# A two-layer hybrid decoder trunk on one core: the inverse norms of K and Q move from VectorE's bit estimate to GpSimd's power

## The chip, the cores and the metric

The kernel runs on one core of a Trainium2 chip. The metric is the time of one execution on the device in microseconds (us). The kernel before takes 1410.69 us, the median of three runs (1410.56 to 1411.05).

The core's engines run side by side, each through a queue of its own in order: TensorE (PE; its weight loads are shown as PEld), VectorE (DVE), ScalarE (ACT), GpSimd (POOL) and SyncE (SP), which here issues the DMAs. They wait for each other by semaphores.

## The reference

Two decoder layers on 512 tokens of width 1024. The first mixes with a state-space scan (SSD) and a stick-breaking attention of 16 heads, the second with an mLSTM; each is followed by a gated feed-forward with a convolution. The change lies in the attention's normalisation of Q and K: every head vector of 64 numbers is divided by its root mean square.

```
def rmsnorm(x, w):
    y = x * rsqrt(mean(x * x, axis=-1) + 1e-6)
    return y * w

heads = lambda t: t.reshape(bsz, seq, 16, 64)
qh = rmsnorm(heads(q), q_norm_w)
kh = rmsnorm(heads(k), k_norm_w)
vh = heads(v)
y_sb = stick_breaking(qh, kh, vh)      # z = qh kh^T / 8, strictly causal
```

## The kernel before, in words

All matrix products are done on float32 split in a high and a low part (`split`, `split_scaled`, and `prefetch` for the weights): ScalarE rounds to the high part, VectorE subtracts to get the remainder (`lo`, `wTl`, `Kl`), and TensorE does three products of the parts. So nearly every product needs VectorE shortly ahead of it.

The attention's projections are done in eight groups of two heads (`kqv`). A group projects the normalised input to K, Q and V, token block by token block (4 blocks of 128), and puts K and Q into two tiles `kqs` of 128x512: four token blocks, each with two heads of K and two of Q, 64 columns a head. Then come the inverse norms, 16 for each of 128 tokens. ScalarE squares (`sq`), VectorE sums each 64 columns (`ss`, 128x16), adds the epsilon, and `rsqrt` takes ss to the power -1/2: it shifts the bits of ss as an integer, subtracts from a constant, and does three Newton steps of three instructions each, twelve instructions of 128x16 on VectorE. VectorE multiplies the two kqs tiles with the result `f`, TensorE transposes them (`tt<-cc,kqs`), ScalarE and VectorE take the transposes apart into `Kh`, `Kl` and `Q`, and one half of Kl is copied to other partitions by a DMA on SyncE's queue.

Two other functions (`rstd`, used by the norms, and `ml_core` of the second layer) already take an inverse root as a GpSimd power with the constant tile `mhalf`, four columns at a time.

What is written down is not what is issued. Every call goes into a `Recorder`. Its `order` then plays the whole program through with a price for each call (`cost`) and a delay for each hand-over between engines (`LATENCY` plus `SLACK`), and the calls are issued in the order of the start times that come out: one fixed order for each engine. A GpSimd call is priced at 60 + 2n ns (n columns), a VectorE call at 69 + about n ns, with 127 ns more to a call on VectorE that needs its result; a hand-over to or from GpSimd costs 150 + 200 ns. So a change in a few calls can move any later instruction on any engine.

`L0_PLAN` says what is woven together in the first layer: groups 0 to 2 stand beside the convolution tiles and the scan's heads (`ssd`), groups 3 to 7 beside the attention (`att`, the function `sb_pair`) of the groups before them. In the attention a pair of heads takes sigmoids on ScalarE, cuts the diagonal blocks with GpSimd's select (`wt<-wt`), runs a scan (`gt`) and a product (`wt`) on VectorE, transposes on TensorE and splits the result (`wTh`, `wTl`).

Weights come through two buffers `raw` and are split into five buffers `hi` and `lo`, so up to five units of weights are ready ahead of TensorE.

Of the kernel before, what the change touches and what calls it, by code (L numbers as in the profile page):

```python
# [15 lines left out]
F32 = mybir.dt.float32  # L16
F32R = mybir.dt.float32r
AF = mybir.ActivationFunctionType
ALU = mybir.AluOpType
# [3 lines left out]
P = 128  # L23
# [411 lines left out]
class Net:  # L435
# [107 lines left out]
        for k in range(KD):  # L543
            self.mm3(ps[:, 0:n], (xs[k][0][:, t], xs[k][1][:, t]), ws[k], k == 0, k == KD - 1)

    def rsqrt(self, y, x, n):

        v, I32 = self.nc.vector, mybir.dt.int32
        b, m = self.sm("nb", n), self.sm("nm", n)
        v.tensor_scalar(y.bitcast(I32), x.bitcast(I32), 1, None, op0=ALU.logical_shift_right)  # L550
        v.tensor_scalar(y.bitcast(I32), y.bitcast(I32), -1, 0x5F3759DF, op0=ALU.mult, op1=ALU.add)
        v.tensor_scalar(m, x, -0.5, None, op0=ALU.mult)
        for _ in range(3):
            v.tensor_tensor(b, y, y, op=ALU.mult)
            v.tensor_tensor(b, b, m, op=ALU.mult)
            v.scalar_tensor_tensor(y, b, 1.5, y, op0=ALU.add, op1=ALU.mult)


    def sumsq_add(self, acc, src, first):
        if first:  # L560
# [203 lines left out]
    def kqv(self, xs, ev, r, pr, dt=None, ws=None):  # L764


        nc, v = self.nc, self.nc.vector
        ws = ws or self.tok_units()
        st = [self.slot("kqs"), self.slot("kqs")]
        V = [self.slot("V", F32R), self.slot("V", F32R)]  # L770
        raw = [self.slot("Vr"), self.slot("Vr")] if dt is not None else None
        for tb in range(NB):
            ps = self.ps()
            self.tok_block(ps, xs, ws, tb)
            o = (tb % 2) * 256
            nc.scalar.copy(st[tb // 2][:, o : o + 256], ps[:, 0:256])
            rt, src = r[:, tb : tb + 1], ps[:, 256:384]
            if raw:
                both = raw[tb // 2][:, o : o + P + 16]
                nc.scalar.copy(both, ps[:, 256 : 384 + 16])  # L780
                src = both[:, 0:P]
                v.scalar_tensor_tensor(dt[:, tb * 16 : tb * 16 + 16], both[:, P : P + 16], rt, self.param("rows", 0, 16), op0=ALU.mult, op1=ALU.add)
            src = self.v3(src, 2)
            vh, vl = (V[tb // 2][:, o : o + 256].rearrange("p (e s c) -> p e s c", e=2, s=2)[:, :, k] for k in range(2))
            nc.scalar.activation(vh, src, AF.Copy, scale=rt)
            v.scalar_tensor_tensor(vl, src, rt, vh.bitcast(F32), op0=ALU.mult, op1=ALU.subtract)
            yield
        ss, f = self.sm("ss", 16), self.sm("f", 16)
        for j in range(2):
            sq = self.slot("sq")  # L790
            nc.scalar.activation(sq, st[j], AF.Square)
            v.tensor_reduce(ss[:, 8 * j : 8 * j + 8], self.v3(sq, 8), axis=AX.X, op=ALU.add)
        v.scalar_tensor_tensor(self.v3(ss, NB), self.v3(ss, NB), 1.0 / 64, ev.unsqueeze(2).broadcast_to([P, NB, 4]),
                               op0=ALU.mult, op1=ALU.add)
        self.rsqrt(f, ss, 16)
        for j in range(2):
            v.tensor_tensor(self.v3(st[j], 8), self.v3(st[j], 8), f[:, 8 * j : 8 * j + 8].unsqueeze(2).broadcast_to([P, 8, 64]), op=ALU.mult)
        yield
        pk, pq = self.ps("tt"), self.ps("tt")
        for k, pt in enumerate((pk, pq)):  # L800
            for tb in range(NB):
                o = (tb % 2) * 256 + k * P
                self.transpose(pt[:, tb * P : (tb + 1) * P], st[tb // 2][:, o : o + P])
        KL, K, Q = [], [], []
        for e in range(2):
            own, other = slice(e * 64, e * 64 + 64), slice(64 - e * 64, P - e * 64)
            kh, kl, q = self.slot("Kh", F32R), self.slot("Kl", F32R), self.slot("Q", F32R)
            nc.scalar.copy(kh[own], pk[own])
            nc.scalar.copy(kh[other], pk[own])
            v.tensor_tensor(kl[own], pk[own], kh[own].bitcast(F32), op=ALU.subtract)  # L810
            nc.sync.dma_start(kl[other].bitcast(F32), kl[own].bitcast(F32))
            KL.append(kl)
            nc.scalar.activation(q[own], pq[own], AF.Copy, scale=self.wqk[own])
            v.scalar_tensor_tensor(q[other], pq[own], self.wqk[own], q[own].bitcast(F32), op0=ALU.mult, op1=ALU.subtract)
            K.append(kh)
            Q.append(q)
        self.kqv_of[pr] = (K, KL, Q, V)
        yield
# [340 lines left out]

    def run(self):  # L1160
        nc = self.nc
        self.mhalf = self.const.tile([P, 8], F32, name="mhalf")
        nc.vector.memset(self.mhalf, -0.5)
        warm = self.slot("warm", F32R)
        nc.gpsimd.memset(warm.bitcast(F32), 0.0)
# [117 lines left out]
        a, b, c = L1_CUTS  # L1283
# [78 lines left out]
```

## Time and profile before

| | |
|---|---|
| median of three runs | 1410.69 us |
| the profiled execution | 1410.06 us |
| its span, from the first to the last instruction | 1408.3 us |
| TensorE busy | 1397.9 us (99%) |
| VectorE busy | 989.2 us (70%) |
| ScalarE busy | 742.3 us (53%) |
| GpSimd busy | 58.9 us (4%) |
| share of the chain that ended last | TensorE 88%, VectorE 5%, ScalarE 3% |

The busy share of an engine is the time in which at least one of its instructions was being executed. VectorE's instructions overlap a little: the next begins before the last has ended. A busy TensorE can still hide short waits, since its instructions are pipelined and their ends are modelled. All lines of the recorded calls have the number of the one line that issues them, L422, so the groups are told apart by the names of their tiles.

### The profile page before, as it was taken

To read this page: it belongs to the slowest core of one execution; us is meant where nothing else is said; L and a number is where in the kernel's file an instruction comes from. 1 tells how busy PE (TensorE), PEld (TensorE's weight loads), DVE (VectorE), ACT (ScalarE), POOL (GpSimd) and SP (SyncE) were. 2 spreads that over 40 slices of the span, in tenths; PEclk is the share of its full clock that TensorE was granted. 3 is DMA by queue.
4 is the path that set the end of the run, shared out by engine and by line. 5 is a ranking of instruction groups with operands and counts; after the bars stand their busy time and mean duration, and the time that the engine had idled before them with its cause. 6 is when DMAs were issued, how large, how long until landed. Compare 5 with 4: busy or idle time off the path is not lost.

```text
span 1408.3 us, 18392 instructions
## 1 busy us (share of the span) xinstructions
PE 1397.9 (99%) x6915; PEld 1170.1 (83%) x6915; DVE 989.2 (70%) x1659; ACT 742.3 (53%) x1229; POOL 58.9 (4%) x140
## 2 busy tenths in 40 slices
PE   9999999999999999999999999999999999999998
PEld 8898999989788888888888898888888888888887
DVE  7999889999987676677623347799767777675221
ACT  7798987886665444444422236685444444443110
POOL 0000001211120000000000000010000000000000
PEclk9999999999999999999999999999999999999999
DMA  6423323234213223323233225232223223223330
GB/s 217 128 76 120 91 61 101 65 91 150 83 31 120 90 90 99 96 90 104 83 98 94 72 76 170 70 109 78 85 90 105 90 90 103 93 86 105 109 102 33
DMA packets 44393, 135.27 MB, mean 96 GB/s; under 512 B 5112, under 2 KB 6136, under 8 KB 44304
## 3 DMA queue, kind: packets, MB, share of 16 engines
q1 hardware_dynamic: 44304, 134.09, 30.5%
q8 instruction: 54, 0.88, 0.3%
q14 instruction: 35, 0.29, 0.1%
HBM read 128.78 MB, written 2.15 MB: 93 GB/s over the span
## 4 chain that ended last, share of the span: by engine, by line
PE 88%; DVE 5%; ACT 3%; issue 3%; DMA 1%; POOL 0%; SPq 0%; DVEq 0%; POOLq 0%; ACTq 0%
PE pj L422 42%; PE yy L422 20%; PE zz L422 17%; PE tt L422 8%; DVE gt L422 1%; DVE wt L422 1%; DVE lo L422 1%; DVE wTl L422 1%; DMA E<-mrow 0%; ACT L422 0%; ACT E L422 0%; ACT Kh L422 0%; POOL wt L422 0%; DMA w<-in_w 0%; ACT Q L422 0%
## 5 line engine op out<-in xcount | busy, mean ns | idle before, releaser
L422 ACT CAST hi<-raw 128x1024 fp32r<-128x1024 f32 (+2 forms) x236 | 234.7, 997 | 269.5 <-PE pj L422 75.9
L422 DVE TENSOR_TENSOR lo<-raw,hi 128x1024 fp32r<-128x1024 f32 (+2 forms) x236 | 272.4, 1156 | 135.3 <-ACT hi L422 135.0
L422 PE MATMUL pj<-xnh,hi 128*128 128x512 f32 x544 | 216.8, 398 | 0.0
L422 PE MATMUL pj<-xnh,lo 128*128 128x512 f32 x544 | 215.9, 397 | 0.0
L422 PE MATMUL pj<-xnl,hi 128*128 128x512 f32 x544 | 215.4, 396 | 0.0
L422 DVE SCALAR_TENSOR_TENSOR c<-u,pp,c 128x511 f32<-128x511 f32 (+2 forms) x212 | 158.0, 748 | 3.5 <-ACT c L422 0.5
L422 PEld LDWEIGHTS pj<-xnh,lo 128*128 128x128 f32 x544 | 102.3, 188 | 22.1
L422 PEld LDWEIGHTS pj<-xnl,hi 128*128 128x128 f32 x544 | 102.3, 188 | 21.4
L422 PEld LDWEIGHTS pj<-xnh,hi 128*128 128x128 f32 x544 | 102.3, 188 | 21.3 <-issue 0.2
L422 PE MATMUL pj<-lo,xnh 128*128 128x384 f32 (+2 forms) x320 | 108.6, 340 | 0.0
L422 PE MATMUL pj<-hi,xnl 128*128 128x384 f32 (+2 forms) x320 | 107.2, 335 | 0.0
L422 PE MATMUL pj<-hi,xnh 128*128 128x384 f32 (+2 forms) x320 | 106.8, 338 | 0.0
L422 PE MATMUL zz<-xnh,lo 128*128 128x512 f32 x224 | 88.4, 394 | 0.0
L422 PE MATMUL yy<-xnh,lo 128*128 128x512 f32 x224 | 88.4, 394 | 0.0
L422 PE MATMUL yy<-xnh,hi 128*128 128x512 f32 x224 | 88.3, 394 | 0.0
L422 PE MATMUL zz<-xnh,hi 128*128 128x512 f32 x224 | 88.3, 394 | 0.0
L422 PE MATMUL yy<-xnl,hi 128*128 128x512 f32 x224 | 88.2, 394 | 0.0
L422 PE MATMUL zz<-xnl,hi 128*128 128x512 f32 x224 | 88.2, 394 | 0.0
L422 ACT CAST sh<-c 128x512 fp32r<-128x512 f32 x44 | 27.3, 620 | 113.5 <-DVE c L422 113.5
L422 ACT ACTIVATE c<-c 128x512 f32<-128x512 f32 x56 | 35.3, 631 | 96.9 <-DVE c L422 96.8
L422 ACT ACTIVATE c<-u,pp 128x512 f32<-128x512 f32 x100 | 81.4, 816 | 1.2 <-DVE u L422 0.9
L422 DVE TENSOR_TENSOR u<-pj,rb 128x512 f32<-128x512 f32 x44 | 30.4, 691 | 48.4 <-PE pj L422 44.2
(363 smaller groups left out, 2977.2 us busy)
## 6 DMA issues: line engine op xcount, KB each, us to landing
raw<-in_w SPq DMA_DIRECT2D x184, 512.0 KB, 3.6
raw<-in_w SPq DMA_DIRECT2D x44, 384.0 KB, 3.1
h<-in_xT SPq DMA_DIRECT2D x16, 256.0 KB, 4.4
E<-acsd SPq DMA_DIRECT2D x16, 256.0 KB, 4.0
raw<-in_w SPq DMA_DIRECT2D x8, 264.0 KB, 2.7
Kl<-Kl SPq DMA_DIRECT2D x16, 128.0 KB, 2.2
E<-mrow SPq DMA_DIRECT2D x8, 256.0 KB, 5.4
out_h<-h SPq DMA_DIRECT2D x8, 256.0 KB, 2.0
```

The source lines that it names most:

```text
L422: getattr(getattr(nc, c.engine), c.method)(*(r(a) for a in c.args), **{k: r(v) for k, v in c.kw.items()})
```

## The change

The method `rsqrt` is taken out, the one call of it is replaced by a single GpSimd instruction, and the constant tile becomes 16 columns wide.

```diff
-    def rsqrt(self, y, x, n):
-
-        v, I32 = self.nc.vector, mybir.dt.int32
-        b, m = self.sm("nb", n), self.sm("nm", n)
-        v.tensor_scalar(y.bitcast(I32), x.bitcast(I32), 1, None, op0=ALU.logical_shift_right)
-        v.tensor_scalar(y.bitcast(I32), y.bitcast(I32), -1, 0x5F3759DF, op0=ALU.mult, op1=ALU.add)
-        v.tensor_scalar(m, x, -0.5, None, op0=ALU.mult)
-        for _ in range(3):
-            v.tensor_tensor(b, y, y, op=ALU.mult)
-            v.tensor_tensor(b, b, m, op=ALU.mult)
-            v.scalar_tensor_tensor(y, b, 1.5, y, op0=ALU.add, op1=ALU.mult)
...
-        self.rsqrt(f, ss, 16)
+        nc.gpsimd.tensor_tensor(f, ss, self.mhalf, op=ALU.pow)
...
-        self.mhalf = self.const.tile([P, 8], F32, name="mhalf")
+        self.mhalf = self.const.tile([P, 16], F32, name="mhalf")
```

The order of the instructions changes with it from the first group on. VectorE's queue in group 0, before, from the sum of squares with its epsilon (ss): lo is a remainder of weights, V a remainder of the values, nm and nb are scratch of the Newton steps.

```order
L422 SCALAR_TENSOR_TENSOR ss_339<-ss_339,ev_376 128x16
L422 TENSOR_TENSOR lo_405<-raw_342,hi_385 128x1024
L422 SCALAR_TENSOR_TENSOR V_395<-Vr_299,rstd_381,V_395 128x2x64
L422 SCALAR_TENSOR_TENSOR V_398<-Vr_318,rstd_381,V_398 128x2x64
L422 TENSOR_SCALAR f_423<-ss_339 128x16
L422 TENSOR_SCALAR nm_425<-ss_339 128x16
L422 TENSOR_SCALAR f_423<-f_423 128x16
L422 TENSOR_TENSOR nb_432<-f_423 128x16
L422 TENSOR_TENSOR nb_432<-nb_432,nm_425 128x16
L422 SCALAR_TENSOR_TENSOR dtx_401<-Vr_299,rstd_381,pp 128x16
```

The same place on VectorE in the changed kernel:

```order
L422 SCALAR_TENSOR_TENSOR ss_339<-ss_339,ev_376 128x16
L422 TENSOR_TENSOR lo_405<-raw_342,hi_385 128x1024
L422 SCALAR_TENSOR_TENSOR V_395<-Vr_299,rstd_381,V_395 128x2x64
L422 SCALAR_TENSOR_TENSOR V_398<-Vr_318,rstd_381,V_398 128x2x64
L422 TENSOR_TENSOR kqs_295<-kqs_295,f_410 128x512
L422 TENSOR_TENSOR kqs_315<-kqs_315,f_410 128x512
L422 SCALAR_TENSOR_TENSOR dtx_401<-Vr_299,rstd_381,pp 128x16
```

The scaling of K and Q, which stood 21 rows behind the first instruction of rsqrt, now stands directly where that one stood, and reads f from GpSimd.

TensorE's queue in group 0, before, where the transposes of K and Q stand; pj_430 is the first projection tile behind the transposes of the norm's rep, pj_491 the second:

```order
L422 MATMUL pj_430<-xnh_237,lo_329 128x512
L422 MATMUL pj_491<-xnh_106,hi_366 128x512
L422 MATMUL pj_491<-xnl_114,hi_366 128x512
L422 MATMUL pj_491<-xnh_106,lo_379 128x512
L422 MATMUL pj_491<-xnh_116,hi_366 128x512
L422 MATMUL tt_499<-cc,kqs_295 128x128 x2
L422 MATMUL tt_503<-cc,kqs_295 128x128 x2
L422 MATMUL pj_491<-xnl_134,hi_366 128x512
L422 MATMUL tt_499<-cc,kqs_315 128x128 x2
L422 MATMUL tt_503<-cc,kqs_315 128x128 x2
```

The same transposes on TensorE in the changed kernel, where the first of these projection tiles is called pj_428:

```order
L422 MATMUL pj_352<-xnh_237,lo_307 128x512
L422 MATMUL pj_428<-xnh_106,hi_305 128x512
L422 MATMUL pj_428<-xnl_114,hi_305 128x512
L422 MATMUL pj_428<-xnh_106,lo_329 128x512
L422 MATMUL pj_428<-xnh_116,hi_305 128x512
L422 MATMUL tt_435<-cc,kqs_295 128x128 x2
L422 MATMUL tt_440<-cc,kqs_295 128x128 x2
L422 MATMUL tt_435<-cc,kqs_315 128x128 x2
L422 MATMUL tt_440<-cc,kqs_315 128x128 x2
L422 MATMUL pj_428<-xnl_134,hi_305 128x512
```

They have moved ahead by one whole projection tile of 24 matmuls, and all eight now stand together.

VectorE's queue in group 6 in the changed kernel, in the attention, where least stands between the sum and the scaling (gt is the scan, wt the product behind it):

```order
L422 SCALAR_TENSOR_TENSOR gt_3552<-gt_3552,cc 128x511
L422 SCALAR_TENSOR_TENSOR ss_3471<-ss_3471,ev_376 128x16
L422 TENSOR_TENSOR wt_3557<-wt_3557,gt_3552 128x511
L422 TENSOR_TENSOR kqs_3385<-kqs_3385,f_3571 128x512
L422 TENSOR_TENSOR kqs_3483<-kqs_3483,f_3571 128x512
L422 TENSOR_TENSOR lo_3592<-raw_3523,hi_3567 128x1024
```

Before, 22 instructions stood between ss and kqs in this group, twelve of them those of rsqrt; now it is one.

## Rows read from the trace of the kernel before

**Rows 1.** The page's first part: busy us of each engine, share, instructions.
```profile
PE 1397.9 (99%) x6915; PEld 1170.1 (83%) x6915; DVE 989.2 (70%) x1659; ACT 742.3 (53%) x1229; POOL 58.9 (4%) x140
```
**Rows 2.** Busy time by stretch: us, engines, PEclk (granted clock), DMA share, GB/s.
```profile
150.00:200.00 50.00, 50.00 (x344) 47.21 (x343) 40.77 (x83) 45.14 (x90) 0.00 (x0) 1.00 0.25 75
200.00:250.00 50.00, 49.14 (x310) 44.87 (x309) 48.45 (x102) 38.90 (x82) 7.84 (x16) 1.00 0.27 80
250.00:300.00 50.00, 48.95 (x295) 44.07 (x295) 48.01 (x101) 38.65 (x77) 6.48 (x12) 1.00 0.26 78
300.00:350.00 50.00, 50.00 (x285) 44.54 (x285) 46.91 (x86) 36.27 (x69) 8.40 (x13) 1.00 0.42 130
350.00:400.00 50.00, 48.21 (x268) 39.69 (x267) 46.69 (x77) 33.72 (x64) 7.60 (x16) 1.00 0.25 76
```
**Rows 3.** Groups on GpSimd: xcount | busy us, mean ns | idle before, releasers.
```profile
L422 POOL TENSOR_TENSOR f<-ss,mhalf 128x4 f32<-128x4 f32 x8 | 8.1, 1006 | 63.9 <-DVE ss L422 63.9
L422 POOL TENSOR_SCALAR_AFFINE_SELECT E<-E 128x512 f32<-128x512 f32 x8 | 6.2, 778 | 61.5 <-ACT E L422 61.5
L1354 POOL MEMSET const-float32-0.0<- 128x1 f32 x1 | 0.1, 98 | 0.3 <-issue 0.3
```
**Rows 4.** Tile f: min/median/max ns, first and last start.
```profile
L422 DVE TENSOR_TENSOR nb<-f x24: 153/174/177, 30.6 to 349.5; 128x16 f32<-128x16 f32 x24
L422 DVE TENSOR_TENSOR kqs<-kqs,f x16: 684/690/791, 35.9 to 351.2; 128x512 f32<-128x512 f32 x16
```
**Rows 5.** Timeline of VectorE in group 0: start us, us.
```profile
28.14 0.17 DVE L422 SCALAR_TENSOR_TENSOR ss<-ss,ev 128x16 f32<-128x16 f32 x1
...
30.14 0.17 DVE L422 TENSOR_SCALAR f<-ss 128x16 int32<-128x16 int32 x1
30.22 0.17 DVE L422 TENSOR_SCALAR nm<-ss 128x16 f32<-128x16 f32 x1
30.35 0.17 DVE L422 TENSOR_SCALAR f<-f 128x16 int32<-128x16 int32 x1
30.56 0.17 DVE L422 TENSOR_TENSOR nb<-f 128x16 f32<-128x16 f32 x1
```
**Rows 6.** Timeline of TensorE in group 0.
```profile
29.52 0.60 PE L422 MATMUL tt<-cc,rep 128*128 128x128 f32 x4
...
32.04 0.39 PE L422 MATMUL pj<-xnl,hi 128*128 128x512 f32 x1
...
37.57 0.60 PE L422 MATMUL tt<-cc,kqs 128*128 128x128 f32 x4
```
**Rows 7.** Timeline around a power in the second layer.
```profile
909.27 0.17 DVE L422 TENSOR_SCALAR ss<-ss 128x4 f32<-128x4 f32 x1
...
909.52 1.01 POOL L422 TENSOR_TENSOR f<-ss,mhalf 128x4 f32<-128x4 f32 x1 [0.39 <-DVE ss L422]
...
910.56 0.16 DVE L422 TENSOR_TENSOR f<-f,r 128x4 f32<-128x4 f32 x1 [0.41 <-POOL f L422]
```
**Rows 8.** Groups on VectorE by shape, 175 to 352 us.
```profile
L422 DVE TENSOR_TENSOR lo<-raw,hi 128x768 fp32r<-128x768 f32 x18 | 17.1, 949 | 0.0
L422 DVE TENSOR_TENSOR lo<-raw,hi 128x1024 fp32r<-128x1024 f32 x10 | 12.1, 1215 | 0.0
L422 DVE TENSOR_TENSOR_SCAN gt<-gt,cc 128x511 f32<-128x511 f32 x10 | 12.1, 1213 | 0.0
L422 DVE TENSOR_TENSOR wTl<-tt,wTh 128x384 fp32r<-128x384 f32 x19 | 10.4, 547 | 0.8 <-ACT wTh L422 0.8
...
L422 DVE TENSOR_TENSOR wt<-wt,gt 128x511 f32<-128x511 f32 x10 | 6.9, 688 | 0.1
```
**Rows 9.** Waits of SyncE's queue (total us, times, longest); ScalarE's table loads.
```profile
SPq L422 <- DVE Kl L422: 36.3, 13, 12.3
...
L422 ACT ACT_TABLE_LOAD x27 | 34.6, 1283 | 5.0 <-DVE c L422 3.8 <-PEq L1354 0.8
```

## The prediction

> **What bounds the kernel now.** I read the page's busy shares first. TensorE is busy for 1397.9 of 1408.3 us, VectorE for 989.2 [rows 1]. So a change can give back little: TensorE's own work stays, and only its gaps can close. Next the stretches of the span. The eight K/Q/V groups that the change touches end between 36 and 352 us, with the scaling kqs [rows 4]; five of them lie in the attention, three ahead of it. From 150 to 200 us, the last stretch ahead of the attention, TensorE is never idle, and VectorE is busy for 40.8 of 50 us. From 200 to 350 us, the attention, both are near their limit: VectorE is busy for 48.45, 48.01 and 46.91 of 50 us, and TensorE lacks 0.86, 1.05 and 0 us; another 1.79 us is missing between 350 and 400, after the last of the touched places [rows 2]. The granted clock is 1.00 in all of them, so no gain or loss is put down to it. The gaps that a relieved VectorE could close are therefore about 1.9 us, or 3.7 us with those after 350 us.
>
> **What is removed.** Twelve instructions of 128x16 per group on VectorE, 96 in all, of about 174 ns each [rows 4]. Their busy time, 96 x 0.17 = 16.5 us, is not what they take from the queue. In the first group the shift starts at 30.14, the next rows at 30.22, 30.35 and 30.56 us [rows 5]: an instruction that is followed by an independent one holds the queue for 0.08 us, one whose successor needs its result for 0.21 us. All twelve at 0.21 would be 2.5 us per group, all at 0.08 1.0 us. The chains are partly interleaved with other work, so I take 1.5 us per group: 12 us in all, 7.5 of it in the five groups of the attention.
>
> **What is added.** Eight powers on GpSimd, each 128x16, and two hand-overs. The trace has powers of 128x4 and none wider: 1006 ns as the mean of the eight in the second layer [rows 3]. That leaves the width's price open, and everything hangs on it. Lower bound: the price is per instruction, 1.0 us. Upper bound: it is per column, 4 x 1.006 = 4.0 us. Between them: a GpSimd fill of one column takes 98 ns and a select of 128x512 takes 778 ns for 128 times as many columns as the power has [rows 3]. So neither starting an instruction nor moving columns explains 1006 ns; the arithmetic of the power does, and it is done per column. (1006 - 98) / 4 = 227 ns a column, and 98 + 16 x 227 = 3.73 us. With a larger fixed part it is somewhat less; I take 3.6 us and keep 1.0 and 4.0 as ends.
>
> The Trainium skill (GPSIMD Engine Reference, section 2.1) gives the software dispatch as one indirect call, tens of cycles per instruction. The fill row agrees (98 ns for all of it), and by that rule too most of the 1006 ns would be column work.
>
> The hand-overs are short. In the second layer the sum ends at 909.27 + 0.17 = 909.44, the power starts at 909.52, ends at 910.53, and VectorE's next use of it starts at 910.56 [rows 7]: 0.08 and 0.03 us. So the path from the sum to the scaling of K and Q is 3.6 + 0.1 = 3.7 us (1.1 at the lower bound).
>
> **What hides it.** VectorE runs its queue in order, and the order is made by the recorder, which prices the power at 60 + 2 x 16 = 92 ns. It therefore puts the scaling (kqs) soon after the sum. Between the two stand, by the changed order: group 0: one 1024-wide remainder and two V remainders, 30.14 - 28.31 = 1.8 us [rows 5]; group 1: one 1024-wide, 1.1; group 2: a 768-wide, two state products and a mask product, about 2.4; group 3: a 768-wide and a 255-wide product, 1.2; group 4: two wT remainders and a short scan, 1.4; group 5: a wT remainder and a 383-wide scan, 1.4; group 6: one 511-wide product, 0.6; group 7: a 511-wide scan and a wT remainder, 1.6 (durations from [rows 8], less 0.08 for each instruction, since the next one starts that much before it ends; widths that are not shown pro rata). That is 11.5 us of cover for 8 x 3.7 = 29.6 us, so VectorE stands idle for about 18 us, of which 12.3 us (18.5 - 6.2) fall into groups 3 to 7. At the lower bound it is 0.5 us, all of it in group 6.
>
> Who stands behind the waiting kqs on VectorE: the remainders and scans that feed TensorE's projections and products. On GpSimd the selects behind the power (groups 3 to 5) wait for it too, but the products that use them stand behind kqs on VectorE anyway, so they add nothing. On SyncE's queue the copies of Kl move ahead of up to three loads; they hang on kqs, and the queue already stands 36.3 us for them in 13 waits [rows 9]. A load behind them can now be late by as much as kqs is. Five split units of weights lie ready ahead of it, 24 matmuls each, so I cost this at nothing; if the cover is gone, it is the 0.9 us a group of the last rival. ScalarE gets one more table load in the changed order (28 against 27), 1.28 us each [rows 9]; with ScalarE busy for 742.3 us [rows 1] I cost it at nothing, and at 1.3 us if it falls on the path.
>
> **The sum.** Groups 0 to 2: VectorE has room, so only TensorE's transposes of K and Q matter. In the first group the order is the same up to there: the changed order puts them nine matmuls behind the transposes of rep, that is where the matmul of 32.04 us stands now, instead of 37.57 us [rows 6]. The sum ends at 28.31 [rows 5], the first kqs runs from 32.0 to 32.7, the second from 32.6 to 33.3. TensorE wants the second at 32.04 + 0.35 = 32.4 and waits about 0.9 us. No wait arises below a power of about 2.7 us. Group 1 has less cover and a like place: 0.9. Group 2 has 0.6 more: 0.3. Together 2.1 us.
> Groups 3 to 7: VectorE loses 12.3 us to waits and gets back 7.5, net +4.8 us, in a stretch where it has 6.6 us of idle time (150 - 143.4) [rows 2]. Part of the net falls into that idle time; I pass 0.6 of it on to TensorE: 2.8 us.
> Sum: +4.9 us against the profiled execution, 1410.06 us (span 1408.3 and 1.8 around it). The median of the three runs is 1410.69, 0.6 above; on it the forecast is 1415.6 us.
>
> **Rivals.**
> *The power costs the same at any width.* Then kqs hardly waits, VectorE is relieved of 12 us and the attention's gaps shrink. For it: no row shows how the price grows, and 1006 ns is far above the other instructions of its engine. Against: the 98 ns fill. Even then only the 1.9 us between 200 and 350 and part of the rest can come back: -2.0 us, 1408.7 us. This is the case that is not slower; it decides from a power under about 2 us.
> The Trainium skill (GPSIMD Engine Reference, section 3.1) gives about 2.6 cycles per element and partition for an elementwise operation on GpSimd. By it twelve more columns would add an estimated 26 ns, and the power would be 1.03 us, which is this rival; but by it the four columns of now would take 9 ns, and the row has 1006, so it does not hold for a power.
> *A wide power, but covered.* The recorder's slack carries it: other waits in the queue (for ScalarE's halves) fall together with those for the power, and TensorE's order has enough ahead of the transposes. For it: TensorE's transposes of K and Q hardly wait now. Against: those have just been moved up by 5.5 us in the first group. About +0.8 us: 1411.5.
> *The waits add up.* In the attention the transposes wait 0.9 us in each of the five groups as well, and the idle time of VectorE absorbs nothing: 2.1 + 4.8 + 4.5 = 11.4, and the table load 1.3: 1423.4 us. For it: 48.45 of 50 busy. Against: work of the next group stands beside it.
>
> **Chances.** Forecast 0.55, power of one price 0.22, covered 0.13, added up 0.10. The range 1407.8 to 1423.0 takes in the two ends of the power's price. 0.2% (2.8 us) is about what a measurement of this kernel can tell from no change. Slower by more: the forecast but for its lowest part, and the last rival: 0.63. Within: most of the one-price case, the covered case and that lowest part: 0.28. Faster by more needs more than the gaps of 200 to 350 us: 0.09.
>
> **What would show it.** In the new profile: the mean of f<-ss,mhalf 128x16 (3.5 to 3.8 us right; about 1.0 makes the first rival true); VectorE idle before kqs for GpSimd's f, some 18 us in eight waits, the largest in group 6, nearly 3 us; VectorE's busy time down by about 16 us; TensorE waiting for kqs in the first group by about 0.9 us near 33 us; the stretches from 200 to 350 us longer by about 3 us in all, the feed-forward parts as long as before. If the power is wide and the kernel is still not slower, then my step from VectorE's waits to TensorE's is wrong; if it is narrow and the kernel is slower, the new order is to blame, not the power.

## The result, and the profile after

The changed kernel takes 1427.74 us (median of four runs, 1423.76 to 1428.39) against 1410.62 for the kernel before: a ratio of 1.0117, 95% interval 1.0103 to 1.0131. It is slower by 17 us, above the range of the prediction (1407.8 to 1423.0). The profiled execution took 1428.07 us. The fastest of the four, 1423.76 us, is the only one with a mean granted clock of 1.000; the others have 0.996 to 0.999.

The page's first part, busy us of each engine (compare [rows 1]):

```profile
PE 1403.4 (98%) x6915; PEld 1172.6 (82%) x6915; DVE 980.6 (69%) x1563; ACT 745.4 (52%) x1230; POOL 87.0 (6%) x148
```

VectorE lost its 96 instructions, but only 8.6 us of busy time, not the 16 I had named: they overlapped with their neighbours. GpSimd has 28 us more. Its groups by shape (xcount | busy us, mean ns), which answer to [rows 3]:

```profile
L422 POOL TENSOR_TENSOR f<-ss,mhalf 128x16 f32<-128x16 f32 x8 | 26.7, 3340 | 81.2 <-DVE ss L422 78.6 <-DMA raw<-in_w 2.5
L422 POOL TENSOR_TENSOR f<-ss,mhalf 128x4 f32<-128x4 f32 x8 | 8.1, 1007 | 65.1 <-DVE ss L422 65.1
```

The wide power takes 3.34 us on average: the price grows with the columns. Who waited for it, in the tables of waits (us in total, times, longest), first VectorE's, then TensorE's:

```profile
DVE kqs L422 <- POOL f L422: 17.2, 8, 2.8
```
```profile
PE tt L422 <- DVE kqs L422: 8.9, 7, 2.3
PE tt L422 <- DVE wt L422: 4.8, 6, 2.3
```
```profile
PEld tt L422 <- DVE kqs L422: 4.9, 4, 2.2
```

VectorE stands idle for 17.2 us before the scaling of K and Q. TensorE stands idle for 8.9 us before the transposes, in groups 0, 1 and 4 to 7 (the waits of PEld, its weight loads, lie in the same places and are not added). In group 3 VectorE's wait of 2.43 us reaches TensorE one step later: TensorE waits 2.27 us, to 223.78 us, for a product wt that stands behind kqs on VectorE. Group 2's wait of 1.27 us shows in no wait of TensorE. Group 6 shows how a wait becomes TensorE's loss. VectorE's timeline there (start us, us, idle before in brackets):

```profile
300.68 0.20 DVE L422 SCALAR_TENSOR_TENSOR ss<-ss,ev 128x16 f32<-128x16 f32 x1
300.89 0.69 DVE L422 TENSOR_TENSOR wt<-wt,gt 128x511 f32<-128x511 f32 x1
304.37 1.29 DVE L422 TENSOR_TENSOR kqs<-kqs,f 128x512 f32<-128x512 f32 x2 [2.79 <-POOL f L422]
```

GpSimd and TensorE at the same place:

```profile
300.97 3.37 POOL L422 TENSOR_TENSOR f<-ss,mhalf 128x16 f32<-128x16 f32 x1
```
```profile
302.44 0.71 PE L422 MATMUL tt<-cc,wt 128*128 128x128 f32 x5
305.12 0.44 PE L422 MATMUL tt<-cc,kqs 128*128 128x128 f32 x2 [1.97 <-DVE kqs L422]
```

VectorE idles 2.79 us for f; TensorE has done all that stands ahead of the transposes by 303.15 us and idles 1.97. What it still had queued covers 0.8 us of the wait, no more.

The stretches that answer to [rows 2] (busy us of PE, PEld, DVE, ACT, POOL, each with its count; granted clock; DMA):

```profile
200.00:250.00 50.00, 45.49 (x282) 41.16 (x282) 41.66 (x72) 38.01 (x77) 13.28 (x17) 1.00 0.24 72
250.00:300.00 50.00, 47.97 (x300) 44.35 (x299) 45.13 (x76) 38.46 (x78) 9.56 (x14) 1.00 0.27 79
300.00:350.00 50.00, 48.03 (x273) 42.27 (x271) 41.66 (x66) 32.50 (x60) 10.39 (x11) 1.00 0.34 109
350.00:400.00 50.00, 46.00 (x244) 37.42 (x242) 44.01 (x73) 32.49 (x59) 11.94 (x17) 0.97 0.29 90
```

TensorE lacks 12.5 us in these four stretches, 3.7 before; VectorE has much more idle time than before and cannot use it. In the last stretch the granted clock is 0.97, a mean over the two levels: it is 0.83 from 360 to 370 us, right after TensorE waited 2.3 us for kqs, and 1.00 in the tens of us beside that. The five powers of the norms mark the stages of the program, and say where the time went: the first two stages are the first layer's mixer with the touched groups and the attention, then come its feed-forward, the second layer's mixer and its feed-forward. Before, the last two stood at 826.88 and 1042.45 us, and the first three were:

```profile
26.41 1.01 POOL L422 TENSOR_TENSOR rstd<-var,mhalf 128x4 f32<-128x4 f32 x1 [25.09 <-DVE var L422]
...
328.12 1.01 POOL L422 TENSOR_TENSOR rstd<-var,mhalf 128x4 f32<-128x4 f32 x1 [5.18 <-DVE var L422]
...
459.86 1.01 POOL L422 TENSOR_TENSOR rstd<-var,mhalf 128x4 f32<-128x4 f32 x1 [42.42 <-DVE var L422]
```

In the changed kernel:

```profile
28.53 1.01 POOL L422 TENSOR_TENSOR rstd<-var,mhalf 128x4 f32<-128x4 f32 x1 [27.21 <-DVE var L422]
...
338.91 1.01 POOL L422 TENSOR_TENSOR rstd<-var,mhalf 128x4 f32<-128x4 f32 x1 [8.20 <-DVE var L422]
...
476.87 1.01 POOL L422 TENSOR_TENSOR rstd<-var,mhalf 128x4 f32<-128x4 f32 x1 [43.73 <-DVE var L422]
...
846.58 1.01 POOL L422 TENSOR_TENSOR rstd<-var,mhalf 128x4 f32<-128x4 f32 x1 [20.30 <-DVE var L422]
...
1062.12 1.01 POOL L422 TENSOR_TENSOR rstd<-var,mhalf 128x4 f32<-128x4 f32 x1 [49.14 <-DVE var L422]
```

From the first to the second mark 310.4 us against 301.7, from the second to the third 138.0 against 131.7: 14.9 us in the two stages with the touched groups and the attention. In them TensorE is idle for 15.2 us, 3.7 before. Another 2.1 us lie ahead of the first mark, at the start, before any changed instruction; five experiments with the same order have that mark at 26.2 to 26.9 us, so the new order is not what makes it; what does is not shown.

### The profile page after: what moved, and what is told of

Read it like the earlier page. It is cut to its first block, busy times and chain, and to the rows that moved or that the text cites. A ratio compares the mean times of both kernels' runs of the same rounds, so it can differ in the third digit from the quotient of the medians.

```text
span 1426.4 us, 18318 instructions
## 1 busy us (share of the span) xinstructions
PE 1403.4 (98%) x6915; PEld 1172.6 (82%) x6915; DVE 980.6 (69%) x1563; ACT 745.4 (52%) x1230; POOL 87.0 (6%) x148
## 4 chain that ended last, share of the span: by engine, by line
PE 82%; DVE 8%; issue 3%; ACT 3%; POOL 2%; DMA 1%; SPq 0%; DVEq 0%; POOLq 0%; ACTq 0%
PE pj L422 37%; PE yy L422 21%; PE zz L422 16%; PE tt L422 8%; POOL f L422 2%; DVE gt L422 2%; DVE wt L422 1%; DVE lo L422 1%; DVE wTl L422 0%; DVE kqs L422 0%; ACT hi L422 0%; DMA w<-in_w 0%; ACT L422 0%; DVE ss L422 0%; DVE Q L422 0%
## 5 line engine op out<-in xcount | busy, mean ns | idle before, releaser
L422 DVE TENSOR_TENSOR lo<-raw,hi 128x1024 fp32r<-128x1024 f32 (+2 forms) x236 | 272.1, 1155 | 136.8 <-ACT hi L422 136.3
L422 PE MATMUL pj<-xnh,hi 128*128 128x512 f32 x512 | 204.2, 399 | 0.0
L422 PE MATMUL pj<-xnh,lo 128*128 128x512 f32 x512 | 203.6, 398 | 0.0
L422 PE MATMUL pj<-xnl,hi 128*128 128x512 f32 x512 | 202.8, 396 | 0.0
L422 PEld LDWEIGHTS pj<-xnh,lo 128*128 128x128 f32 x512 | 96.3, 188 | 20.6
L422 PEld LDWEIGHTS pj<-xnh,hi 128*128 128x128 f32 x512 | 96.4, 188 | 19.9 <-issue 0.2
L422 PEld LDWEIGHTS pj<-xnl,hi 128*128 128x128 f32 x512 | 96.3, 188 | 20.0
L422 PE MATMUL yy<-xnh,lo 128*128 128x512 f32 x256 | 101.5, 397 | 0.0
L422 PE MATMUL yy<-xnh,hi 128*128 128x512 f32 x256 | 101.0, 395 | 0.0
L422 PE MATMUL yy<-xnl,hi 128*128 128x512 f32 x256 | 101.0, 395 | 0.0
L422 PEld LDWEIGHTS pj<-lo,xnh 128*128 128x128 f32 x320 | 60.3, 189 | 1.4
```

Of the source, the lines that this page charges most:

```text
L422: getattr(getattr(nc, c.engine), c.method)(*(r(a) for a in c.args), **{k: r(v) for k, v in c.kw.items()})
```

## The experiments

### The same order with other prices for the power

The recorder's price depends on the shape alone, so the operation can be exchanged with every queue in the same order; in e2_pow8 and e3_pow32, where the width differs, the price is held at that of 16 columns. That holds the reshuffled order fixed and changes only how long GpSimd takes.

**e1_mult.**

```diff
-        nc.gpsimd.tensor_tensor(f, ss, self.mhalf, op=ALU.pow)
+        nc.gpsimd.tensor_tensor(f, ss, self.mhalf, op=ALU.mult)
```

> The changed kernel, every queue in exactly the same order, with the GpSimd power replaced by a GpSimd multiplication of the same operands (the inverse root is left out). Theory 1, the power's duration: TensorE pays for the time that VectorE waits for f, eight waits of 17.2 us in all. A 128x16 multiplication should take under 0.3 us, all eight waits go, and the time falls back to 1410, plus or minus 2 us; VectorE's 12 us of relief is then worth next to nothing. Theory 2, the new order: the reshuffled queues themselves cost the time, so it stays at 1422 us or more.

1410.72 us, ratio 0.9999 (0.999 to 1.0009): the whole loss is gone. The multiplication takes 548 ns on average (0.22 us at the least), nothing waits for it, and group 6 reads as follows on TensorE:

```profile
291.42 0.71 PE L422 MATMUL tt<-cc,wt 128*128 128x128 f32 x5
291.97 0.38 PE L422 MATMUL tt<-cc,kqs 128*128 128x128 f32 x2
```

The transposes of kqs follow at once, 0.55 us after those of wt started; with the power it was 2.68 us. Theory 1 stands: in this order it is the power's duration that makes the changed kernel slower. What the order itself does is asked further down.

**e2_pow8.**

```diff
+        nc.gpsimd.tensor_tensor(f[:, 0:8], ss[:, 0:8], self.mhalf[:, 0:8], op=ALU.pow)
...
```

> Same order as the changed kernel, the power taken on 8 of the 16 columns and used for both halves (the other 8 inverse norms are left out). Theory 1: the power takes some 1.6 to 1.9 us, path 1.9 us against covers of 0.6 to 2.4, so the waits fall from 17.2 to about 5 us and the time is about 1414 us. Theory 2: 1422 us or more, hardly below the changed kernel.

1415.99 us, 1.0035 (1.0022 to 1.0048). The power takes 2.10 us on average, VectorE waits 7.1 us:

```profile
DVE kqs L422 <- POOL f L422: 7.1, 7, 1.5
```

**e3_pow32.**

```diff
+        nc.gpsimd.tensor_tensor(self.v3(f2, 2), ss.unsqueeze(1).broadcast_to([P, 2, 16]),
+                                self.v3(self.mhalf, 2), op=ALU.pow)
```

> Same order as the changed kernel, the power taken on 32 columns (each norm twice), so only its duration grows. Theory 1: 5.5 to 6.5 us a power, 2.2 to 3.2 us more for each of eight waits, and as TensorE pays nearly all of them, 18 to 25 us more: 1446 to 1453 us. Theory 2: VectorE waits longer, but at most a third of it reaches TensorE: below 1436 us.

1456.22 us, 1.0321 (1.0305 to 1.0336); the power takes 5.88 us, VectorE waits 37.4 us:

```profile
DVE kqs L422 <- POOL f L422: 37.4, 8, 5.3
```

It is 3 to 10 us more than I expected. In the long waits the granted clock falls too, to 0.91 to 0.93 as the mean of the four stretches from 200 to 400 us, which lies between the two levels of 1.2 and 2.4 GHz:

```profile
200.00:250.00 50.00, 45.21 (x278) 43.42 (x277) 38.14 (x66) 37.70 (x76) 10.56 (x11) 0.93 0.24 68
...
300.00:350.00 50.00, 45.16 (x237) 39.81 (x237) 40.11 (x63) 32.21 (x59) 10.62 (x8) 0.91 0.29 85
```

In one order, then:

| kernel | power, mean us | VectorE's wait for f, us | time, us | above e1_mult |
|---|---|---|---|---|
| e1_mult | 0.55 (a multiplication) | 0 | 1410.72 | |
| e2_pow8 | 2.10 | 7.1 | 1415.99 | 5.3 |
| changed kernel | 3.34 | 17.2 | 1427.74 | 17.0 |
| e3_pow32 | 5.88 | 37.4 | 1456.22 | 45.5 |

Each us that VectorE waits for the power costs the kernel 0.75, 0.99 and 1.2 us. The rise goes at least in part with the clock: over its whole span e3_pow32 has a mean granted clock of 0.987, e2_pow8 1.000. An estimate from these: the lower level costs e3_pow32 at most 0.013 x 1454.9 = 19 us of its 45.5 (at most, since TensorE also waited in that time). Without them a us of wait costs about 0.7 us there. So a us of wait costs some 0.7 to 1 us in this order, and more where the clock falls.

### Where the wait costs

```diff
+        nc.gpsimd.tensor_tensor(f, ss, self.mhalf, op=ALU.pow if pr < 3 else ALU.mult)     # e6_pow_012
+        nc.gpsimd.tensor_tensor(f, ss, self.mhalf, op=ALU.pow if pr >= 3 else ALU.mult)    # e7_pow_34567
```

**e6_pow_012.**

> The changed kernel's order, the power in groups 0 to 2 (ahead of the attention) and the multiplication in groups 3 to 7 (their inverse roots are left out). My sum had 2.1 us here. Theory 1 (TensorE pays nearly the whole wait): 3 to 4 us over e1_mult, about 1414 us. If groups 0 to 2 hold the larger part of the loss instead: over 1418 us.

1414.06 us, 1.0027 (1.0016 to 1.0038): 3.3 us over e1_mult, about half of VectorE's waits:

```profile
DVE kqs L422 <- POOL f L422: 6.3, 3, 2.8
```

**e7_pow_34567.**

> The counterpart: multiplication in groups 0 to 2, the power in groups 3 to 7, in the attention, where my sum had 2.8 us. Theory 1: the waits of VectorE for f in these groups, 11 us in the changed kernel's trace, reach TensorE nearly whole and some more follows, 11 to 14 us over e1_mult, 1422 to 1425 us. The rival (VectorE's idle time and relief absorb 40% or more, as my sum had it): 1413 to 1417 us.

1423.77 us, 1.0094 (1.0079 to 1.0109): 13.1 us over e1_mult, for this wait on VectorE:

```profile
DVE kqs L422 <- POOL f L422: 10.6, 5, 2.8
```

The marks of the norms put 10.8 us of it into the two stages of the first layer (307.1 and 136.3 us against 298.8 and 133.9 in e1_mult); 1.9 us lie in the second layer's mixer, where nothing differs but the clock: from 950 to 960 us the granted clock is 0.83 in this execution and 1.00 in e1_mult's, with TensorE busy for all 10 us in both: an estimated 0.17 x 10 = 1.7 us. What made it fall in this execution is not shown. The two parts add up to 16.4 of the 17.0 us.

### What VectorE's relief is worth

**e5_mult_newton.**

```diff
+            if getattr(out.base, "name", "").split("_")[0] in ("spare", "nb", "nm"):
+                return 0.0
...
+        nc.gpsimd.tensor_tensor(f, ss, self.mhalf, op=ALU.mult)
+        self.rsqrt(self.sm("spare", 16), ss, 16)
```

> e1_mult with the twelve VectorE instructions of the bit estimate and the Newton steps put back into every group, into a spare tile that nothing reads; every other instruction of every queue keeps its place (the inverse root is left out as in e1_mult). It asks what VectorE's relief is worth by itself. Theory A (the relief is worth nothing, since TensorE's gaps can't close): within 1.5 us of e1_mult, 1409.5 to 1412. Theory B (the relief is worth what my sum credited, 12 us of queue at some 0.6, and the new order ate it up in e1_mult): 1415 to 1419 us.

1416.89 us, 1.0044 (1.0029 to 1.0059), 6.2 us over e1_mult. Theory A falls. By the marks 5.2 us of it lie in the two stages of the first layer. So the relief is worth some 5 to 6 us in this order, and since e1_mult only equals the kernel before, the new order by itself must be about as much worse than the old one: with the twelve instructions in it e5_mult_newton is 6.4 us slower than the kernel before, 4.5 us in the same two stages. These two cancel; I had not priced the second. One reservation: at a price of 0 the twelve stand where no plan put them, so a part of the 5 to 6 us may be their place.

### Orders that know the power's price

**e4_priced.**

```diff
+        if c.kw.get("op") == ALU.pow and n == 16:
+            return 3340.0
```

> The changed kernel with the recorder's price of the 16-column power set from 92 to its measured mean, 3340 ns, so that the order puts the scaling and the transposes later. Theory 1: the waits for f nearly vanish and the time is 1409 to 1413 us; if VectorE's relief is worth something it shows here, as a time below 1409. Theory 2 (any reshuffled order loses against the one of before, which was tuned around): still 1418 us or more.

1412.65 us, 1.0017 (1.0007 to 1.0027). No wait for f is left and the loss shrinks from 17 to 1.8 us, at the upper edge of what I expected. Its ten runs spread from 1411.58 to 1417.28 us, and the slow ones have the lower clock: in the profiled one, 1416.95 us, the granted clock is 0.66 from 940 to 950 us, in the second layer.

**e10_priced_mult.** The order of e4_priced, word for word, with the power replaced and the price of 3340 ns kept:

```diff
-        nc.gpsimd.tensor_tensor(f, ss, self.mhalf, op=ALU.pow)
+        nc.gpsimd.tensor_tensor(f, ss, self.mhalf, op=ALU.mult)
```

> The order of e4_priced, word for word, with a multiplication in place of the power (the inverse root is left out). Theory power: what keeps e4_priced above before is the power itself, selects late behind it on GpSimd; then this is 1406 to 1409 us. Theory order: the order that came out of that price is a poor one; then it stays at 1411 to 1413 us.

1411.1 us, 1.0007 (0.9998 to 1.0016). It lies 1.6 us below e4_priced, in the range of theory order, but the intervals of the two ratios overlap (1.0007 to 1.0027 there). How the 1.8 us of e4_priced divide between the power and the order is not decided.

**e12_price4300.** Against e4_priced:

```diff
-            return 3340.0
+            return 4300.0
```

> e4_priced with the 16-column power priced at 4300 ns, the longest that its trace has, instead of 3340. If e4_priced lost by a price that was still too low: 1406 to 1409 us. If the price is not the matter (no wait for f was left at 3340) and the difference between orders is a lottery of some us, anything from 1408 to 1416.

1407.93 us, 0.998 (0.997 to 0.9989): a little faster than before. VectorE waits 1.2 us for f in all. The time lies in the range of a price that was too low, but e4_priced had no wait for f to lose, so a mere lottery of orders is not excluded.

**e8_halves.**

```diff
+            v.tensor_reduce(h, self.v3(sq, 8), axis=AX.X, op=ALU.add)
+            v.scalar_tensor_tensor(...)                       # epsilon, half by half
+            nc.gpsimd.tensor_tensor(sf[j][:, 8:16], h, self.mhalf[:, 0:8], op=ALU.pow)
...
+        if c.kw.get("op") == ALU.pow and n == 8:
+            return 2100.0
```

> A version that could win: two powers of 8 columns a group, each issued as soon as its half of the sums is there, and priced at 2100 ns in the recorder. If waits for f were all that is lost, 1409 to 1411 us, the same as before; faster than 1408 only if VectorE's relief is worth something. If what the power does to the order and to the selects behind it on GpSimd matters as well (e4_priced stayed 1.8 us above before), 1412 us or more.

1406.15 us, 0.997 (0.9958 to 0.9981): faster than both, by 4.3 us against before. Its stretches:

```profile
200.00:250.00 50.00, 49.77 (x307) 45.40 (x307) 46.55 (x79) 40.48 (x82) 15.36 (x20) 1.00 0.26 77
250.00:300.00 50.00, 49.63 (x303) 45.78 (x302) 45.44 (x78) 39.15 (x76) 14.95 (x15) 1.00 0.30 92
300.00:350.00 50.00, 50.00 (x289) 44.49 (x288) 44.50 (x75) 33.16 (x63) 12.01 (x15) 1.00 0.37 123
350.00:400.00 50.00, 49.57 (x274) 40.72 (x273) 47.62 (x76) 34.73 (x65) 8.14 (x18) 1.00 0.22 71
```

TensorE lacks 1.0 us in the four, 3.7 before: this is about what VectorE's relief can buy once nothing waits for the power. By the marks the two stages with the touched groups are 2.9 us shorter than before; the rest of the gain lies in the second layer's feed-forward (363.4 against 365.9 us), whose work did not change, and is no gain of the power. In group 6 three instructions, two of them added by the new order, now cover the second half's power, where wt stood alone:

```profile
288.42 0.69 DVE L424 TENSOR_TENSOR wt<-wt,gt 128x511 f32<-128x511 f32 x1
289.03 1.22 DVE L424 TENSOR_TENSOR lo<-raw,hi 128x1024 fp32r<-128x1024 f32 x1
290.18 0.74 DVE L424 SCALAR_TENSOR_TENSOR ysl<-c,pp,ysh 128x512 fp32r<-128x512 f32 x1
290.84 0.68 DVE L424 TENSOR_TENSOR kqs<-kqs,sf 128x512 f32<-128x512 f32 x1
```

**e9_halves_76.** Against e8_halves (a half is then priced at 60 + 2 x 8 = 76 ns):

```diff
-        if c.kw.get("op") == ALU.pow and n == 8:
-            return 2100.0
```

> e8_halves with the recorder's old price for the two half powers (76 ns each). It tells apart what made e8_halves fast. Theory price (an order that knows how long the power takes): the scaling stands too early again, VectorE waits several us for the halves in all, 1411 to 1416 us. Theory halves (the first half starts early enough by itself): 1405 to 1408 us.

1422.11 us, 1.0078 (1.0062 to 1.0094), more than either theory said. VectorE's waits for the halves are 18.2 us in 16 times. The price makes the difference of 16 us, not the halving.

**e11_halves_mult.** The order of e8_halves, word for word, with multiplications and the price of 2100 ns kept:

```diff
-            nc.gpsimd.tensor_tensor(sf[j][:, 8:16], h, self.mhalf[:, 0:8], op=ALU.pow)
+            nc.gpsimd.tensor_tensor(sf[j][:, 8:16], h, self.mhalf[:, 0:8], op=ALU.mult)
...
```

> The order of e8_halves with multiplications in place of the half powers (the inverse root is left out). Its trace shows no wait for the halves at all. If the waits are the whole price of a power, the time doesn't move: within 1 us of e8_halves, 1405 to 1407. If the power costs something beside the waits, 1403 us or less.

1405.22 us, 0.9964 (0.995 to 0.9978): 0.9 us below e8_halves, and the two intervals overlap. A power that nobody waits for costs next to nothing.

## Why the prediction was wrong

- **The power's price**: near in size, in part by luck. 3.6 us forecast, 3.34 measured, so the rival of one price at any width falls; but 3.34 lies below the 3.5 to 3.8 that I had named as the sign. The working was off: e2_pow8 and e3_pow32 show a larger fixed part and fewer ns a column, 2.90 us for 16 columns at the shortest, and what it is longer beside VectorE's instructions, 0.44 on average, was not in the sum at all (last section).
- **The cover on VectorE**: right. About 18 us of waits in eight places forecast, 17.2 measured. The largest was forecast in group 6, nearly 3 us; it has 2.79, and so has group 1 (2.6 by my cover).
- **Groups 0 to 2**: 2.1 us forecast, 3.3 measured (e6_pow_012). In group 0 TensorE stood idle for 0.78 us before the transposes, 0.9 forecast.
- **The step that failed**: "Groups 3 to 7: VectorE loses 12.3 us to waits and gets back 7.5, net +4.8 us ... I pass 0.6 of it on to TensorE: 2.8 us." The wait was about right, 10.6 us; what these groups cost was not 2.8 us but 13.1 (e7_pow_34567), 10.8 of it in their two stages. At 0.6 the waits alone would have come to 7.4 us; in fact TensorE paid for every us of them. The step let VectorE's idle time elsewhere in the stretch take up a part of the wait. But a wait in an in-order queue happens at one place. In groups 4 to 7 of the changed kernel TensorE stood right behind the waiting kqs and stopped with it, for 1.2 to 2.3 us in each; in group 3 it stopped for 2.27 us at the product behind kqs. The other half of the step, the credit for the relief, is not what failed: 7.5 x 0.6 = 4.5 us of it stood in the sum, and e5_mult_newton puts the relief of all eight groups at 5 to 6.
- **A term put at nothing**: the new order itself, without a reason given. e5_mult_newton puts it at about 5 to 6 us on the slow side, as much as the relief gives back. Since the two cancel, the waits alone (2.1 + 12.3 on the median of before) would have come to 1425 us.
- **The rivals**: the one nearest was "the waits add up", 1423.4 us, which lay just outside the range that I stated. It had the idle time absorb nothing, which is right; the order it left out too. "Covered" falls, by the waits.
- **The feed-forward parts** were not as long as before, which I had said they would be: 369.7 us instead of 367.0 from the third mark to the fourth, 364.3 instead of 365.9 from the last mark to the end.

What stays open: how much of the 1.8 to 6.5 us between e4_priced, e12_price4300 and e8_halves is the place of the power and how much the accident of an order. No run repeats one price with another order. Nor does a run put the twelve instructions back beside the power, so the relief is measured only where nothing waits.

## What to carry to other kernels

A wait in an in-order queue is not paid out of that engine's idle time elsewhere: at each place where it falls, ask what the engine behind has left to do, and if that is nothing, count the wait in full (here groups 3 to 7 cost as much as their waits, groups 0 to 2 half). Where a planner makes the order from prices, an operation that moves to another engine needs its measured price there before anything else is judged; here the price alone was worth 15 to 20 us, and with a good one the same idea went from 17 us slower to 2.6 us faster, and to 4.3 with the power in two halves. And bring no gain in VectorE's time into such a sum beyond the gaps that the bounding engine still has: 3.7 us were open here, and e8_halves won 2.9 in the two stages.

## What the runs showed of the hardware

**GpSimd's power by width.** The shortest at each width are 1.006 us for 4 columns (kernel before), 1.63 for 8 (e2_pow8), 2.90 for 16 (changed kernel) and 5.43 for 32 (e3_pow32): about 0.375 us fixed and 158 ns a column.

**VectorE lengthens it.** In the changed kernel three of the eight take 2.90 us and the other five 3.37 to 3.82. The long ones start while VectorE runs a remainder lo or a product wt; in group 6 above the product has 0.61 us to go when the power starts, and the power is 0.47 us longer. In group 4 VectorE runs wT remainders, whose one input is in PSUM, and then a scan, and the power is short:

```profile
244.41 2.90 POOL L422 TENSOR_TENSOR f<-ss,mhalf 128x16 f32<-128x16 f32 x1 [5.99 <-DVE ss L422]
```
```profile
244.25 1.14 DVE L422 TENSOR_TENSOR wTl<-tt,wTh 128x512 fp32r<-128x512 f32 x2
245.31 0.41 DVE L422 TENSOR_TENSOR_SCAN gt<-gt,cc 128x127 f32<-128x127 f32 x1
```

The Trainium skill (GPSIMD Engine Reference, section 8) says that GpSimd shares its SBUF interfaces with VectorE and contends with VectorE instructions that have two SBUF inputs. The rows agree: lo and wt have two such inputs, wTl has one. What counts here is the instruction that runs when the power starts: in e7_pow_34567 the power of group 7 starts 0.16 us into a scan with two such inputs and takes 3.74 us, while in group 5 of the changed kernel a like scan begins 0.48 us after the power, which takes 2.90, and the scan its usual 0.95. The multiplication shows the same in group 6: 0.70 us in e1_mult, beside the product, and 0.22 in e5_mult_newton, where the product starts after it. No run was made to isolate it.

**A stage that did not change has another speed.** In the feed-forward of the first layer the matmuls of 512 columns start 231.6 ns apart before and 233.1 in the changed kernel (the mean distance of their starts in the traces). From the third mark of the norms to the fourth the changed kernel and the five experiments with its order word for word need 369.7 us, the kernel before 367.0, e8_halves 367.7. The matmuls are the same in shape, but for 15 that write a PSUM tile of another name and two more between the marks. In the second layer's feed-forward it is the other way round, 364.3 us against 365.9 before. What in the build sets it was not tried.
